# Prompt attention of a hybrid decoder layer: probabilities transposed in 32 by 32 blocks on VectorE and placed by DMAs through DRAM, in place of TensorE transposes

## The chip, the core and the metric

The kernel runs on one core of one Trainium2 chip. TensorE (PE) multiplies; VectorE (DVE), ScalarE (ACT) and GpSimd (POOL) do the rest; SyncE (SP) issues the weight loads. Each engine works through its own list of instructions in order, and semaphores hold an instruction until what it needs is there. The metric is the device time of one launch in microseconds; lower is better. The kernel before takes 1600.82 us (median of three runs, 1600.62 to 1601.08).

## The reference

One decoder layer for 256 prompt tokens and 64 sample tokens (8 sequences of 8). A combined projection gives the gates and inputs of a short convolution, and q, k, v of a sliding-window attention; two output projections, a merge, and a SwiGLU follow. What the change touches is the prompt's attention: 16 query heads, 4 key heads of width 64, in blocks of 128 queries, each of which sees its own block of keys and the one before.

```python
def window_attend(q, k, v, dist, valid, rel_bias, sinks):
    s = jnp.einsum('...qhgd,...shd->...hgqs', q, k).astype(jnp.float32) * (HEAD_DIM ** -0.5)
    bias = rel_bias.astype(jnp.float32)[t5_bucket(dist)]
    ...
    s = jnp.where(valid, s + bias, -jnp.inf)
    sink = sinks.astype(jnp.float32).reshape(N_KV_HEADS, GROUP, 1, 1)
    m = jnp.maximum(jnp.max(s, axis=-1, keepdims=True), sink)
    p = jnp.exp(s - m)
    p = p / (jnp.sum(p, axis=-1, keepdims=True) + jnp.exp(sink - m))
    return jnp.einsum('...hgqs,...shd->...qhgd', p.astype(v.dtype), v)
```

The scores `s` come out with queries on the partitions and keys along the row. The last product sums over keys, so the probabilities have to be turned: keys on the partitions.

## The kernel before

**Projections.** Every weight matrix is read once, in tiles of 4 x 128 rows by 256 columns. SP loads a tile as float32 (`wraw`, four buffers); ACT rounds it to the high part `whi` (L129) and VectorE subtracts to get the low part `wlo` (L130), three buffers of each. `product` (L172) then issues 24 matmuls on the tile: high part by the high and low parts of the activations, low part by the high part, 320 tokens wide. The projections run in the order q (four tiles per 256 columns), then four rounds of C, H, B (the convolution's inputs), then the gates and the output projections, then the feed-forward part.

**Side work.** After each tile `product` calls `tick`, which advances a generator by one step. While C, H and B run, that generator is the attention: its instructions are put between the tiles' matmuls on PE and between the `whi` and `wlo` on ACT and VectorE. The framework orders each engine's list by its own estimates, so that neighbours in the program may stand some places apart.

**The prompt's attention.** `prompt_attention` (L624) goes over eight units u0 to u7. A unit is one key head, two of its query heads and both query blocks: four 128 by 128 tiles of scores. A round of its loop takes two ticks. Per unit:

- `bias_load` (L530): GpSimd loads the relative biases (256 KB) one unit ahead.
- `prompt_scores` (L540): six matmuls into two PSUM banks, then four VectorE operations that add the biases. In the first query block each key row is used once; in the second, keys of the block before and of the own block are each masked out for half of the positions, and exactly one of the two is valid at each place, so the two are merged by a maximum into one 128 by 128 tile.
- `prompt_softmax` (L566): maximum on VectorE, four exponentials with their sums on ACT.
- `prompt_norm` (L585), one round later: division by the sums, four VectorE operations.
- `prompt_pt` (L591), one round after that: PE transposes the four tiles into the PSUM bank `pp`; ACT copies the first block's half into `pT`; VectorE multiplies the second block's half by the two masks `sides` (keys of the block before, keys of the own block), which undoes the merge and takes it to SBUF as well.
- `prompt_pv` (L605), for four units at a time: twelve matmuls by the values `vn` into two PSUM banks `po`, whose results ACT and VectorE split into the high and low rows of `at_t`.

```python
            if i >= 3 and (i - 3) % 4 == 3:
                for n in (i - 5, i - 3):
                    kv, gp = units[n]
                    prompt_pv(kv // 2, gp, (pts.pop(n - 1), pts.pop(n)))
```

The sample tokens' attention (L649) follows in the same generator and takes over the prompt's buffers. GpSimd also multiplies the convolution's rows by the norm (L829, L830), prepares the next rows (L811, L812) and keeps the state (L818, L819).

`vT` and `kT` (L277, L278) hold the transposed values and keys of all tokens. Their prompt part is read for the last time before the first unit (`kv_natural`, `keys_twice`); of `kT` the sample part is read later.

Of the kernel before, what the change touches and what calls it, by code (L numbers as in the profile page):

```python
# [8 lines left out]
F32 = mybir.dt.float32  # L9
F32R = mybir.dt.float32r  # L10
AF = mybir.ActivationFunctionType
# [5 lines left out]
TP, NB, TS = 256, 8, 8  # L17
T = TP + NB * TS
DC = 1024
NH, NKV, HD, GRP = 16, 4, 64, 4  # L20
DKV = NKV * HD
WIN = 128
# [4 lines left out]
P = 128  # L27
# [25 lines left out]
def hybrid_layer(ctx: ExitStack, tc: tile.TileContext, a: dict, o: list):  # L53
    nc = tc.nc
# [12 lines left out]
    dr = ctx.enter_context(tc.tile_pool(name="dr", bufs=1, space=bass.MemoryType.DRAM))  # L67
# [4 lines left out]
    def ps_aux(name):  # L72
        return aux[0].tile([P, 512], F32, tag="aux", name=name)
# [3 lines left out]
    def u(s):  # L77
        uid[0] += 1
        return f"{s}_{uid[0]}"
# [139 lines left out]
    ident = cst.tile([P, P], F32, name="ident")  # L219
# [57 lines left out]
    kT = zz.tile([P, 2, T], F32, name="kT")  # L277
    vT = zz.tile([P, 2, T], F32, name="vT")  # L278
    vn = [zz.tile([P, DKV], F32, name=f"vn{t}") for t in range(3)]
# [198 lines left out]
    pr = pr_p.enter_context(tc.tile_pool(name="pr", bufs=1, side="right"))  # L478
# [6 lines left out]
    sides = pr.tile([P, 2, WIN], F32, name="sides")  # L485
# [12 lines left out]
    def kv_natural(t):  # L498
        t0, tn = TOK[t]
        pk = ps_aux(u("pk"))  # L500
        for j in range(2):
            nc.tensor.transpose(pk[:tn, j * P:(j + 1) * P], vT[:, j, t0:t0 + tn], ident)
        if t > 0:
            for j in range(2):
                nc.tensor.transpose(pk[:tn, 256 + j * P:256 + (j + 1) * P], kT[:, j, t0:t0 + tn], ident)
        nc.vector.tensor_copy(vn[t][:tn, :], pk[:tn, 0:DKV])
        if t > 0:
            kn = pr.tile([P, 4, WIN], F32, tag="s", name=u("kn"), bufs=3).rearrange("p g k -> p (g k)")[:, :DKV]
            nc.vector.tensor_copy(kn[:tn, :], pk[:tn, 256:512])
            if t == 1:  # L510
                nc.gpsimd.dma_start(nk_p[0, 0].rearrange("t h d -> t (h d)"), kn)
                nc.gpsimd.dma_start(nv_p[0, 0].rearrange("t h d -> t (h d)"), vn[1])
            else:
                for dst, s in ((nk_s, kn), (nv_s, vn[2])):
                    nc.gpsimd.dma_start(
                        dst[0, :, WIN - TS:WIN].rearrange("b t h d -> b t (h d)"), s[:tn, :]
                    )
# [22 lines left out]
    def prompt_scores(kv, gp, bias):  # L540

        j, par = kv // 2, kv % 2
        s = pr.tile([P, 4, WIN], F32, tag="s", name=u("s"), bufs=3)
        ps1, ps0 = ps_aux(u("ps1")), ps_aux(u("ps0"))
        for gi in range(2):
            q = q2(j * 4 + gp * 2 + gi, par)
            for i in range(2):  # L550
                nc.tensor.matmul(
                    ps1[:, gi * 256:(gi + 1) * 256], q[:, WIN:2 * WIN], k2[:, kv, i], start=i == 0, stop=i == 1
                )
            nc.tensor.matmul(
                ps0[:, gi * 256:(gi + 1) * 256].rearrange("p (two k) -> p two k", two=2), q[:, 0:WIN],
                k2[:, kv, :, 0:WIN], start=True, stop=True,
            )
        w = pr.tile([P, 2, 2 * WIN], F32, tag="w", name=u("w"), bufs=1)
        nc.vector.tensor_add(w, ps1.rearrange("p (g k) -> p g k", g=2), flip(bias))
        nc.vector.tensor_max(s[:, 2:4], w[:, :, 0:WIN], w[:, :, WIN:2 * WIN])  # L560
        p0 = ps0.rearrange("p (g two k) -> p g two k", g=2, two=2)
        nc.vector.tensor_add(s[:, 0:2], p0[:, :, 0], flip(bias[:, :, 0:WIN]))
        nc.vector.tensor_add(s[:, 0:2], p0[:, :, 1], s[:, 0:2])
        return s

    def prompt_softmax(kv, gp, s):  # L566
# [15 lines left out]
        nc.scalar.activation(es, es, AF.Exp)  # L582
        return den, es

    def prompt_norm(s, den, es):  # L585
        nc.vector.tensor_add(den, den, es)
        nc.vector.reciprocal(den, den)
        for n in range(4):
            nc.vector.tensor_scalar(s[:, n], s[:, n], den[:, n // 2, n % 2:n % 2 + 1], None, op0=ALU.mult)

    def prompt_pt(s):  # L591
        pt = pr.tile([P, 3, 2 * WIN], F32, tag="pT", name=u("pT"), bufs=4)
        pp = ps_aux(u("pp"))
        for n in range(4):
            nc.tensor.transpose(pp[:, n * WIN:(n + 1) * WIN], s[:, n], ident)
        nc.scalar.activation(pt[:, 0, :], pp[:, 0:256], AF.Copy)
        for b in range(2):
            nc.vector.tensor_mul(
                pt[:, 1 + b, :].rearrange("p (g q) -> p g q", g=2),
                pp[:, 256:512].rearrange("p (g q) -> p g q", g=2),  # L600
                sides[:, b:b + 1].to_broadcast([P, 2, WIN]),
            )
        return pt

    def prompt_pv(j, gp, pts):  # L605
        po = ps_aux(u("po"))
        steps = ((0, 0, 0, True, True), (1, 0, 1, True, False), (1, 1, 2, False, True))
        for b, t, kb, st_, sp_ in steps:
            for par in range(2):
                kv = j * 2 + par  # L610
                nc.tensor.matmul(
                    po[par * 64:(par + 1) * 64, b * 256:(b + 1) * 256],
                    vn[t][:, kv * HD:(kv + 1) * HD], pts[par][:, kb, :], start=st_, stop=sp_,
                )
        for g in range(2):
            src = po.rearrange("p (b g s j) -> p g b s j", b=2, g=2, j=JS)[:, g]
            ch = j * 4 + gp * 2 + g
            two_to(*(x(ch)[:, 0:TP // JS, :].rearrange("p (b s) j -> p b s j", b=2) for x in (at_h, at_l)), src)
# [4 lines left out]

    def prompt_attention():  # L624
        units = [(j * 2 + par, gp) for j in range(2) for gp in range(2) for par in range(2)]
        bias, sc, sm, pts = {}, {}, {}, {}
        bias[0] = bias_load(*units[0])
        for i in range(len(units) + 3):
            if i < len(units):
                if i + 1 < len(units):  # L630
                    bias[i + 1] = bias_load(*units[i + 1])
                sc[i] = prompt_scores(*units[i], bias.pop(i))
                yield
                sm[i] = prompt_softmax(*units[i], sc[i])
            if i >= 3 and (i - 3) % 4 == 3:
                for n in (i - 5, i - 3):
                    kv, gp = units[n]
                    prompt_pv(kv // 2, gp, (pts.pop(n - 1), pts.pop(n)))
            if 0 <= i - 2 < len(units):
                pts[i - 2] = prompt_pt(sc.pop(i - 2))  # L640
            yield
            if 0 <= i - 1 < len(units):
                prompt_norm(sc[i - 1], *sm.pop(i - 1))
            if i >= len(units):
                yield

# [151 lines left out]
    for cp in range(4):  # L798
        c_sb = []
        ps = in_pair(O_C + cp * CW, "C")  # L800
        for c in range(2):
            t = tmp("ta", "csb")
# [472 lines left out]
```

## Time and profile before

| what | value |
|---|---|
| median of three runs | 1600.82 us |
| span of the profiled execution, first to last instruction | 1598.6 us |
| instructions | 26406 |
| granted TensorE clock, mean over the span | 0.998 |
| bytes moved by DMAs | 258.13 MB |
| share of the 16 DMA engines' span taken by GpSimd's queue | 1.3% |
| landing time of a 512 KB weight tile, median | 3.8 us |

The profile is one execution; of it the page gives the span, from the first instruction to the last, which lies 2.2 us under the median of the timed runs. Five columns of engines appear in it: PE for the matmuls, PEld for the loading of the stationary operand, DVE, ACT and POOL. "L186" is line 186 of the kernel. An engine's row shows the instruction's operands as out<-in by the program's names, its shapes, and in square brackets how long the engine had been idle and what ended that. PSUM and SBUF operands aren't told apart in the rows. Matmuls overlap, so what one of them costs is read from the distance between the starts of neighbours, not from its duration.

### The profile page before, as it was taken

The page shows a single profiled execution, that of the slowest core. Times are in us where ns is not written, and L with a number is a line of the kernel's source. Part 1 is how long each engine was busy: PE and PEld are TensorE (multiplying, and loading weights), DVE is VectorE, ACT ScalarE, POOL GpSimd, SP SyncE. Part 2 cuts the span into 40 slices and gives each one's busy share as a digit, 9 for nine tenths or more (in the row PEclk, how much of TensorE's full clock was granted, in tenths as well). Part 3 has the DMA queues.
Part 4 walks back from the last instruction along what each step waited for, and adds up shares of the span by engine and source line. Part 5 has one row for each costly group of instructions (what it writes and reads, how often), then busy time and mean ns, then how long its engine had stood idle before and what let it go on. Part 6 is the DMA issues. An engine that isn't in the chain of part 4 may idle for free.

```text
span 1598.6 us, 26406 instructions
## 1 busy us (share of the span) xinstructions
PE 1590.2 (99%) x10957; PEld 1554.8 (97%) x10957; DVE 884.0 (55%) x1315; ACT 650.6 (41%) x928; POOL 78.3 (5%) x123
## 2 busy tenths in 40 slices
PE   9999999999999999999999999999999999999998
PEld 9999999999999999999999999998888999999887
DVE  7879565445555545556555555553444455555556
ACT  7555433433333334444333333333333334444443
POOL 1101311000000003320000000000000000000000
PEclk9999999999999999999999999999999999999999
DMA  7554546545444444444445454455555445545552
GB/s 271 178 169 138 185 145 195 169 156 156 157 157 158 158 158 158 156 154 155 157 159 159 158 158 156 154 155 162 156 157 158 157 158 158 158 156 154 184 180 93
DMA packets 74399, 258.13 MB, mean 161 GB/s; under 512 B 8552, under 2 KB 11928, under 8 KB 74152
## 3 DMA queue, kind: packets, MB, share of 16 engines
q1 hardware_dynamic: 71880, 249.86, 49.4%
q0 software_dynamic: 1968, 5.90, 1.3%
q8 instruction: 86, 1.41, 0.4%
q10 hardware_dynamic: 432, 0.69, 0.1%
q14 instruction: 33, 0.27, 0.0%
HBM read 253.30 MB, written 5.08 MB: 162 GB/s over the span
## 4 chain that ended last, share of the span: by engine, by line
PE 99%; DVE 0%; ACT 0%; DVEq 0%; issue 0%
PE fu L186 18%; PE fg L186 18%; PE dn L970 9%; PE ga L186 7%; PE wo L186 7%; PE gc L186 7%; PE dn L978 6%; PE B L186 3%; PE C L186 3%; PE H L186 3%; PE q L186 3%; PE ya L186 3%; PE yc L186 3%; PE dl L974 2%; PE kv L376 2%; PE dn L1125 1%
## 5 line engine op out<-in xcount | busy, mean ns | idle before, releaser
L130 DVE TENSOR_TENSOR wlo<-wraw,whi 128x1024 fp32r<-128x1024 f32 (+1 forms) x460 | 561.7, 1222 | 585.4 <-ACT whi L129 470.0
L129 ACT ACTIVATE whi<-wraw 128x1024 fp32r<-128x1024 f32 (+1 forms) x460 | 485.5, 1056 | 720.4 <-PE fu L186 129.4
L186 PE MATMUL fu<-hh_t,whi 128*128 128x320 f32 x704 | 205.1, 301 | 0.0
L186 PE MATMUL fu<-hl_t,whi 128*128 128x320 f32 x704 | 205.1, 301 | 0.0
L186 PE MATMUL fg<-hl_t,whi 128*128 128x320 f32 x704 | 205.1, 301 | 0.0
L186 PE MATMUL fg<-hh_t,whi 128*128 128x320 f32 x704 | 205.1, 301 | 0.0
L186 PE MATMUL fu<-hh_t,wlo 128*128 128x320 f32 x704 | 158.9, 301 | 0.0
L186 PE MATMUL fg<-hh_t,wlo 128*128 128x320 f32 x704 | 158.9, 301 | 0.0
L970 PE MATMUL dn<-a_t,whi 128*128 128x512 f32 x640 | 155.4, 382 | 0.0
L186 PEld LDWEIGHTS fu<-hh_t,whi 128*128 128x128 f32 x704 | 131.8, 187 | 0.0
L186 PEld LDWEIGHTS fg<-hh_t,whi 128*128 128x128 f32 x704 | 131.8, 187 | 0.0
L186 PEld LDWEIGHTS fu<-hl_t,whi 128*128 128x128 f32 x704 | 131.8, 187 | 0.0
L186 PEld LDWEIGHTS fg<-hl_t,whi 128*128 128x128 f32 x704 | 131.8, 187 | 0.0
L970 PEld LDWEIGHTS dn<-a_t,whi 128*128 128x128 f32 x640 | 115.5, 187 | 16.3 <-issue 0.9
L186 PEld LDWEIGHTS fu<-hh_t,wlo 128*128 128x128 f32 x704 | 116.2, 187 | 0.0
L186 PEld LDWEIGHTS fg<-hh_t,wlo 128*128 128x128 f32 x704 | 116.2, 187 | 0.0
L978 PEld LDWEIGHTS dn<-a_t,wlo 128*128 128x128 f32 x640 | 97.7, 188 | 6.9
L978 PE MATMUL dn<-a_t,wlo 128*128 128x320 f32 x640 | 103.4, 301 | 0.0
L186 PE MATMUL wo<-m_l,whi 128*128 128x320 f32 x256 | 74.6, 301 | 0.0
L186 PE MATMUL ga<-xl_t,whi 128*128 128x320 f32 x256 | 74.6, 301 | 0.0
L186 PE MATMUL gc<-xl_t,whi 128*128 128x320 f32 x256 | 74.6, 301 | 0.0
L186 PE MATMUL wo<-m_h,whi 128*128 128x320 f32 x256 | 74.6, 301 | 0.0
(312 smaller groups left out, 2659.0 us busy)
## 6 DMA issues: line engine op xcount, KB each, us to landing
wraw<-in_w_in_dram SPq DMA_DIRECT2D x128, 512.0 KB, 3.8
wraw<-in_w_gate_dram SPq DMA_DIRECT2D x88, 512.0 KB, 3.7
wraw<-in_w_up_dram SPq DMA_DIRECT2D x88, 512.0 KB, 3.7
wraw<-in_w_down_dram SPq DMA_DIRECT2D x88, 512.0 KB, 3.7
wraw<-in_w_o_dram SPq DMA_DIRECT2D x32, 512.0 KB, 3.8
wraw<-in_w_conv_out_dram SPq DMA_DIRECT2D x16, 512.0 KB, 3.7
wraw<-in_w_attn_out_dram SPq DMA_DIRECT2D x16, 512.0 KB, 3.6
wraw<-in_w_kv_dram SPq DMA_DIRECT2D x6, 512.0 KB, 7.5
```

Of the source, the lines that this page charges most:

```text
L129: last["hi"] = nc.scalar.activation(hi, src, AF.Copy)
L130: last["lo"] = nc.vector.tensor_sub(lo, src, hi.bitcast(F32))
L186: last["mm"] = nc.tensor.matmul(turns(fives(ps[c][:, :T])), w[:, k, c * P:(c + 1) * P], turns(x(kc)), start=(kc == 0 and i == 0), stop=(kc ...
L376: last["mm"] = nc.tensor.matmul(turns(fives(ps[c][:, :T])), w[:, k, c * P:(c + 1) * P], turns(x(kc)), start=(kc == 0 and m == 0), stop=(kc ...
L970: nc.tensor.matmul(turns(placed(ps[c])), parts[k][0][:, cs], turns(a_move(k)), start=k == 0, stop=False)
L974: nc.tensor.matmul(low, a_low(k), parts[k][0], start=k == 0, stop=k == nf - 1 and c0 < E0)
L978: last["mm"] = nc.tensor.matmul(turns(placed(ps[c])[:, :, 0:JT]), parts[k][1][:, cs], turns(a_move(k)[:, :, 0:JT]), start=False, stop=k == ...
L1125: nc.tensor.matmul(turns(placed(ps[c])[:, :, JR:]), held[k][0][:, cs], turns(a_move(k)[:, :, JR:]), start=k == 0, stop=k == nf - 1,)
```

## The change

The transposes leave PE. `prompt_norm` now ends with one VectorE block transpose of the unit's four tiles: each 32 by 32 block is turned in place, into the first part of `vT`, which is free by then and serves as the one scratch of all units. A block that belongs to keys 32b to 32b+31 and queries 32a to 32a+31 then stands on the partitions of the queries' group a; it has to move to the partitions of group b. `blocks_out` does this by GpSimd's DMAs: the scratch goes to a DRAM buffer `scr` (256 KB, two buffers), and four loads, one for each group b of 32 partitions, bring it back into `pT` as 128 keys by 4 groups of 32 queries for each of the four tiles (runs of 512 bytes).

`prompt_sides` replaces the PSUM-to-SBUF step: the first block's half is used where it landed, and the second half is multiplied by the two masks in SBUF, once into `pm` (for every second pair of units into the free prompt part of `kT`) and once in place. `prompt_pv` reads the operand as groups of 32 queries.

The loop has one round more (`+ 4` for `+ 3`): the masks come two rounds after the normalization, and a group of value matmuls one round later than before. The scores' buffers `s` go from three to two, the `pT` buffers from four to six. Line numbers from L582 on are shifted: the normalization's division is L596, the block transpose L598, the store to DRAM L588, the loads L590, the masks L614 and L615, the value matmuls L624.

```diff
-            kn = pr.tile([P, 4, WIN], F32, tag="s", name=u("kn"), bufs=3).rearrange("p g k -> p (g k)")[:, :DKV]
+            kn = pr.tile([P, 4, WIN], F32, tag="s", name=u("kn"), bufs=2).rearrange("p g k -> p (g k)")[:, :DKV]
...
-        s = pr.tile([P, 4, WIN], F32, tag="s", name=u("s"), bufs=3)
+        s = pr.tile([P, 4, WIN], F32, tag="s", name=u("s"), bufs=2)
...
+    def blocks_out(dst, src):
+
+        scr = dr.tile([P, 4, dst.shape[2]], F32, tag=f"scr{dst.shape[2]}", name=u("scr"), bufs=2)
+        nc.gpsimd.dma_start(scr, src)
+        for b in range(4):
+            nc.gpsimd.dma_start(dst[32 * b:32 * b + 32], scr[:, b].rearrange("(a i) m -> i a m", a=4))
+
     def prompt_norm(s, den, es):
         nc.vector.tensor_add(den, den, es)
         nc.vector.reciprocal(den, den)
         for n in range(4):
             nc.vector.tensor_scalar(s[:, n], s[:, n], den[:, n // 2, n % 2:n % 2 + 1], None, op0=ALU.mult)
-
-    def prompt_pt(s):
-        pt = pr.tile([P, 3, 2 * WIN], F32, tag="pT", name=u("pT"), bufs=4)
-        pp = ps_aux(u("pp"))
-        for n in range(4):
-            nc.tensor.transpose(pp[:, n * WIN:(n + 1) * WIN], s[:, n], ident)
-        nc.scalar.activation(pt[:, 0, :], pp[:, 0:256], AF.Copy)
-        for b in range(2):
-            nc.vector.tensor_mul(
-                pt[:, 1 + b, :].rearrange("p (g q) -> p g q", g=2),
-                pp[:, 256:512].rearrange("p (g q) -> p g q", g=2),
-                sides[:, b:b + 1].to_broadcast([P, 2, WIN]),
-            )
+        x = vT.rearrange("p c t -> p (c t)")[:, :4 * WIN].rearrange("p (b m) -> p b m", b=4)
+        nc.vector.transpose(
+            x.rearrange("p b (n j) -> p n b j", n=4), s.rearrange("p n (b k) -> p n b k", b=4)
+        )
+        pt = pr.tile([P, 4, 4 * 32], F32, tag="pT", name=u("pT"), bufs=6)
+        blocks_out(pt, x)
         return pt
+
+    def prompt_sides(n, pt):
+        last2 = pt[:, :, 64:].rearrange("p a (g j) -> p a g j", g=2)
+        if n % 4 < 2:
+            pm = pr.tile([P, 4, 64], F32, tag="pm", name=u("pm"), bufs=2)
+        else:
+            pm = kT[:, n % 2, 0:TP].rearrange("p (a m) -> p a m", a=4)
+        parts = [
+            sides[:, b].rearrange("p (a j) -> p a j", a=4).unsqueeze(2).to_broadcast([P, 4, 2, 32]) for b in range(2)
+        ]
+        nc.vector.tensor_mul(pm.rearrange("p a (g j) -> p a g j", g=2), last2, parts[1])
+        nc.vector.tensor_mul(last2, last2, parts[0])
+        return pt[:, :, 0:64], pt[:, :, 64:], pm
...
                 nc.tensor.matmul(
-                    po[par * 64:(par + 1) * 64, b * 256:(b + 1) * 256],
-                    vn[t][:, kv * HD:(kv + 1) * HD], pts[par][:, kb, :], start=st_, stop=sp_,
+                    po[par * 64:(par + 1) * 64, b * 256:(b + 1) * 256].rearrange("p (g a j) -> p a g j", g=2, a=4),
+                    vn[t][:, kv * HD:(kv + 1) * HD], pts[par][kb].rearrange("p a (g j) -> p a g j", g=2),
+                    start=st_, stop=sp_,
                 )
...
-        bias, sc, sm, pts = {}, {}, {}, {}
+        bias, sc, sm, turned, pts = {}, {}, {}, {}, {}
         bias[0] = bias_load(*units[0])
-        for i in range(len(units) + 3):
+        for i in range(len(units) + 4):
...
-            if i >= 3 and (i - 3) % 4 == 3:
-                for n in (i - 5, i - 3):
+            if i >= 4 and i % 4 == 3:
+                for n in (i - 6, i - 4):
                     kv, gp = units[n]
                     prompt_pv(kv // 2, gp, (pts.pop(n - 1), pts.pop(n)))
-            if 0 <= i - 2 < len(units):
-                pts[i - 2] = prompt_pt(sc.pop(i - 2))
             yield
+            if 0 <= i - 3 < len(units):
+                pts[i - 3] = prompt_sides(i - 3, turned.pop(i - 3))
             if 0 <= i - 1 < len(units):
-                prompt_norm(sc[i - 1], *sm.pop(i - 1))
+                turned[i - 1] = prompt_norm(sc.pop(i - 1), *sm.pop(i - 1))
```

## The prediction

> **What bounds the kernel now.** I read the chain of waits and the engines' shares first, since they say whether any edit off the matrix engine can count.
>
> ```profile
> PE 1590.2 (99%) x10957; PEld 1554.8 (97%) x10957; DVE 884.0 (55%) x1315; ACT 650.6 (41%) x928; POOL 78.3 (5%) x123
> PE 99%; DVE 0%; ACT 0%; DVEq 0%; issue 0%
> ```
>
> The chain that ended last is matmul after matmul. Time leaves the kernel only where PE is given less work, and enters only where PE is made to wait. The next view splits the stretch in which the prompt's attention is woven into the projections (columns: PE, PEld, DVE, ACT, POOL busy).
>
> ```profile
> 100.00:140.00 40.00, 40.00 (x295) 39.99 (x294) 38.62 (x104) 22.23 (x64) 7.18 (x17) 1.00 0.55 170
> 140.00:160.00 20.00, 20.00 (x151) 18.70 (x150) 16.76 (x44) 9.94 (x29) 0.00 (x0) 1.00 0.35 114
> ```
>
> PE is full, and between 100 and 140 us VectorE is full too (38.62 of 40). Its 55% over the whole program hides that. VectorE also makes the low part of every weight tile (`wlo`, L130), without which PE cannot go on. The cover between the two is read from one tile, in the timeline (start, duration, engine, line):
>
> ```profile
> 110.32 1.06 ACT L129 ACTIVATE whi<-wraw 128x1024 fp32r<-128x1024 f32 x1 [2.98 <-PE H L186]
> 111.42 1.23 DVE L130 TENSOR_TENSOR wlo<-wraw,whi 128x1024 fp32r<-128x1024 f32 x1
> 118.93 0.39 PE L186 MATMUL B<-xh_t,whi 128*128 128x320 f32 x1
> ```
>
> Three buffers are turned over, so this tile is B's first, used from 118.93 on. Its low part was ready at 112.65, and its eight leading matmuls use only the high part (8 x 0.14 = 1.1 us): 7.4 us of cover. VectorE may be that late before PE notices.
>
> **The change part by part.** *PE, removed.* Each of the 8 units (4 heads-by-query-block tiles each; u0 to u7) gave PE four transposes:
>
> ```profile
> 163.73 0.58 PE L186 MATMUL H<-xh_t,wlo 128*128 128x320 f32 x3
> 164.15 0.60 PE L595 MATMUL pp<-ident,s 128*128 128x128 f32 x4
> 164.50 0.39 PE L186 MATMUL H<-xh_t,whi 128*128 128x320 f32 x1
> 164.73 0.31 PE L186 MATMUL H<-xl_t,whi 128*128 128x320 f32 x1
> 164.87 0.30 PE L186 MATMUL H<-xh_t,whi 128*128 128x320 f32 x1
> L595 PE MATMUL pp<-ident,s x32: 270/272/331, 110.7 to 164.5; 128*128 128x128 f32 x32
> ```
>
> Without the group, H's first matmul would start at 164.15 and its second 0.14 us later, at 164.29; it started at 164.73. A group costs 0.44 us, and 32/4 = 8 groups cost 3.5 us. All of it is on the path, so 3.5 us is also the most that can be won.
>
> *PE, altered.* The value matmuls (L611) now read their moving operand in runs of 32 numbers. The projections in the rows above read in runs of 4 and go at 0.14 us per 320 columns, so I take nothing; the bound above is a doubling of
>
> ```profile
> 142.43 2.81 PE L611 MATMUL po<-pT,vn 128*64 128x256 f32 x24
> ```
>
> twice, 5.5 us. *ACT* loses eight copies from PSUM; ACT was half idle, so nothing.
>
> *VectorE, added.* A block transpose of 128x512 per unit, which no row shows. The nearest are operations that read as many numbers:
>
> ```profile
> L571 DVE TENSOR_REDUCE mx<-s 128x4 f32<-128x512 f32 x8 | 5.5, 682 | 0.1
> L560 DVE TENSOR_TENSOR s<-w 128x256 f32<-128x256 f32 x8 | 3.5, 434 | 0.0
> L598 DVE TENSOR_TENSOR pT<-pp,sides 128x256 f32<-128x256 f32 x14 | 5.3, 415 | 0.0
> L130 DVE TENSOR_TENSOR wlo<-wraw,whi 128x1024 fp32r<-128x1024 f32 x18 | 22.0, 1223 | 4.1 <-ACT whi L129 3.8
> ```
>
> I take 0.7 us; below, 0.42 (as for half the numbers), above, 1.22 (as for twice). The two mask products cost as much from SBUF (434 ns) as from PSUM (415). So VectorE gets 8 x 0.7 = 5.6 us more in a stretch where it has 4.6 us free (60 minus 38.62 and 16.76).
>
> The Trainium skill, VectorE: DVE Perf Modes, section "The three transpose paths", speaks against the change: it lists 390 ns on TensorE and 311 on VectorE for 128x128 in bf16 and advises TensorE for a full 128x128 transpose. An estimate from that page is 4 x 311 = 1.24 us a unit, which would put the sum at the third case below; the trace's four TensorE transposes in 0.44 us disagree with the page's 4 x 390 ns, and no row shows the VectorE one.
>
> *GpSimd, added.* Per unit a 256 KB store to DRAM and, after it has landed, four 64 KB loads, on the queue that also carries the bias loads. Columns: KB each, us from issue to landing; then the issue's own ns.
>
> ```profile
> bias<-e_scr POOLq DMA_DIRECT2D x8, 256.0 KB, 4.1
> kf<-in_cache_kt_dram POOLq DMA_DIRECT2D x4, 256.0 KB, 5.0
> bias_s<-e_scr POOLq DMA_DIRECT2D x1, 68.0 KB, 2.9
> out_dram<-kn POOLq DMA_DIRECT2D x1, 64.0 KB, 3.6
> L511 POOL DMA_DIRECT2D out_dram<-kn x1 | 0.6, 553 | 0.0
> ```
>
> I take 4.1 for the store, 0.57 per issue and 3.6 for a load: from the end of the transpose to the last block in place 4.1 + 3 x 0.57 + 3.6 = 9.4 us, and 4.1 + 4 x 0.57 = 6.4 us of the queue. Bounds: 2.9 for loads that meet no queue, 5.0 for every landing as for the four `kf` loads in a row. A round of the loop takes PE two tiles and one set of scores, 2 x 3.36 + 0.71 = 7.4 us, and the masks come two rounds after the transpose, so in the middle the 9.4 us are mostly covered. They are not at the end, where nothing but the queue separates the last units. VectorE's instructions from unit 7's normalization on stood before as
>
> ```order
> L586 TENSOR_TENSOR den_1971<-den_1971,es_1972 128x4
> L587 RECIPROCAL den_1971<-den_1971 128x4
> L589 TENSOR_SCALAR s_1926<-s_1926,den_1971 128x128 x4
> L130 TENSOR_TENSOR wlo_2119<-wraw_2116,whi_2118 128x1024
> L598 TENSOR_TENSOR pT_2032<-pp_2033,sides 128x256 x2
> L130 TENSOR_TENSOR wlo_2177<-wraw_2174,whi_2176 128x1024
> ```
>
> and stand now (s_1816 is u6, s_1917 u7; vT the scratch; pT_2040 and pT_2087 their placed blocks)
>
> ```order
> L598 STREAM_TRANSPOSE vT<-s_1816 128x4x4x32
> L615 TENSOR_TENSOR pT_1910<-pT_1910,sides 128x4x64
> L593 TENSOR_TENSOR den_1962<-den_1962,es_1963 128x4
> L130 TENSOR_TENSOR wlo_2127<-wraw_2124,whi_2126 128x1024
> L594 RECIPROCAL den_1962<-den_1962 128x4
> L596 TENSOR_SCALAR s_1917<-s_1917,den_1962 128x128 x4
> L598 STREAM_TRANSPOSE vT<-s_1917 128x4x4x32
> L130 TENSOR_TENSOR wlo_2187<-wraw_2184,whi_2186 128x1024
> L130 TENSOR_TENSOR wlo_2217<-wraw_2214,whi_2216 128x1024
> L614 TENSOR_TENSOR kT<-pT_2040,sides 128x256
> ```
>
> Behind the second transpose, which must wait until u6's store has left the one scratch, stand the `wlo` of B's second round; behind u6's mask, which must wait for u6's loads, stand the next. On GpSimd's queue the order is now
>
> ```order
> L588 DMA scr_2041<-vT 128x512
> L590 DMA pT_2040<-scr_2041 32x4x128 x4
> L588 DMA scr_2088<-vT 128x512
> L590 DMA pT_2087<-scr_2088 32x4x128 x4
> L832 COPY g_494<-ue_2156 128x2
> ```
>
> so u7's store goes out only when u6's four loads are issued.
>
> *The walk to the end of it.* In VectorE's timeline before, the stretch from H's third `wlo` to unit 7's scores, and the idle in it:
>
> ```profile
> 105.10 1.22 DVE L130 TENSOR_TENSOR wlo<-wraw,whi 128x1024 fp32r<-128x1024 f32 x1
> 113.06 0.17 DVE L586 TENSOR_TENSOR den<-den,es 128x4 f32<-128x4 f32 x1 [0.42 <-ACT es L582]
> 115.27 1.22 DVE L130 TENSOR_TENSOR wlo<-wraw,whi 128x1024 fp32r<-128x1024 f32 x1 [0.40 <-ACT whi L129]
> 144.94 0.16 DVE L586 TENSOR_TENSOR den<-den,es 128x4 f32<-128x4 f32 x1 [0.44 <-ACT es L582]
> 149.86 1.22 DVE L130 TENSOR_TENSOR wlo<-wraw,whi 128x1024 fp32r<-128x1024 f32 x1 [1.79 <-ACT whi L129]
> 151.00 0.68 DVE L559 TENSOR_TENSOR w<-ps,bias 128x512 f32<-128x512 f32 x1
> ```
>
> It is 45.9 us with 3.05 idle, 42.85 of work. Now six transposes come in (4.2), and four copies of value results (1.3), one pair of masks (0.65) and one `wlo` (1.13) move behind it: 44.0, plus waits for u0's loads of about 1.6 us (its masks stand two `wlo` behind u1's transpose). Unit 7's scores are then added at 105.1 + 45.6 = 150.7, as late as before although PE has saved time. The 8.9 us of work that follow in the order bring u6's transpose to about 160, ending 160.7. Then: store landed 164.9; u7's transpose ends 165.6; u6's loads issued by 167.2, u7's store landed 171.3, its last load 171.3 + 1.7 + 3.6 = 176.6; a mask, a `wlo` and a mask more, 178.6.
>
> PE without any wait: B's second round began at 168.00 and its value matmuls at
>
> ```profile
> 168.00 0.30 PE L186 MATMUL B<-xh_t,whi 128*128 128x320 f32 x1
> 171.51 2.81 PE L611 MATMUL po<-pT,vn 128*64 128x256 f32 x24
> ```
>
> which now stand two tiles later: 171.5 + 6.7 - 3.5 = 174.7, and the part that reads u7's masks comes 16 of the 24 matmuls (1.8 us) later, 176.5. PE waits 178.6 - 176.5 = 2.1 us. On the way, B's first `wlo` ends at 166.8 where PE wants it at 168.0 - 3.5 + 1.1 = 165.6, 1.2 us late; that wait is part of the 2.1, since it moves PE by as much. The sum: 1598.6 - 3.5 + 2.1 = 1597.2 against the profile's own span, and with the 2.2 us that the median of 1600.82 lies above the span, 1599.4 us. At both ends of the unknown prices: landings of 5.0 lengthen the tail by 0.9 + 0.9 + 1.4 and u5's loads ahead of it by 2.3, so 7.6 us of wait and 1604.9; the slow transpose adds 7 x 0.54, so 1603.2; the short prices leave no wait, 1597.3.
>
> **The rivals.** *All hidden.* Loads of 2.9, stores of 3.6 and a transpose of 0.42 shorten the tail by 0.5 + 0.5 + 0.7 + 0.6, more than 2.1: 1597.3. For it: `bias_s`; against: `kf`, and VectorE's fullness. The Trainium skill, DMA: Bandwidth & Descriptors, section "Anatomy of one DMA", fits 2.0 us plus bytes/436e3, an estimate of 2.6 us for 256 KB; by that rule this case holds. The trace's 4.1 disagrees.
>
> *VectorE and the queue become the bound.* With a transpose of 1.0 us or more, or landings near 5.0 (four loads in a row look like `kf`), the low parts come late from C's second round on, and PE loses 6 to 9 us: about 1605, slower. It decides from a loss of 3.5 + 3.2 on.
>
> *The strided value matmuls run at half rate*: 1599.4 + 5.5 = 1604.9. Against it stand the projections' runs of 4.
>
> **How the numbers follow.** Forecast 0.45, all hidden 0.24, VectorE and queue bound 0.27, strided 0.04. A change of 0.2% is 3.2 us, about what a measurement of this kernel can tell. The forecast's own range, 1597.8 to 1603.5, lies within that; all hidden is just beyond it in 0.20 of its 0.24; the last two are slower. Faster 0.20, same 0.49, slower 0.31. The range 1597.2 to 1605 takes in the gain's limit and one slow price, not both.
>
> **What would show it.** No L595 on PE, and tiles that follow each other without the 0.44 us. A STREAM_TRANSPOSE near 0.7 us. VectorE waiting for the loads before u0's, u6's and u7's masks; PE waiting near 165 and before the last value matmuls, 2 us in all. VectorE fuller than 38.62 of 40 from 100 to 140. I am wrong if PE waits for `wlo` already before 150 us, if its waits exceed 6 us, or if a store and its loads take less than 8 us.

## The result, and the profile after

The change makes the kernel slower by some 5 us, about 0.4%; the forecast was 1599.4 us.

| kernel | timed runs, us | span of the profiled run |
|---|---|---|
| before | 1600.87 median (1600.09 to 1601.08) | 1598.6 |
| changed | 1604.42, 1604.99, 1605.63, 1607.44, 1611.77 | 1605.7 |
| ratio | 1.0038, 95% interval 1.0027 to 1.0049 | |

A sixth timing of the changed kernel, 4216.09 us, is a disturbed run and is left out of what follows; with it the median is 1606.54, without it 1605.63. The profiled run is the one of 1607.44.

First the page's shares, then its chain of waits.

```profile
PE 1591.2 (99%) x10925; PEld 1553.2 (97%) x10925; DVE 887.1 (55%) x1323; ACT 647.4 (40%) x920; POOL 100.9 (6%) x163
PE 95%; DMA 2%; POOL 1%; issue 1%; DVE 1%; ACT 0%; DVEq 0%; POOLq 0%
```

PE has lost its 32 transposes (10957 to 10925), VectorE has eight instructions more. The chain, which before was PE to 99%, now runs 5% of the span over DMAs, VectorE and GpSimd: for 1300 of its 1600 us the program is as it was, and in the attention it hangs on the new way through DRAM. The view of PE's waits (total, times, longest; the one at the start of the program is left out) says how often:

```profile
PE C L186 <- DVE wlo L130: 2.1, 1, 2.1
PE B L186 <- DVE wlo L130: 2.0, 2, 1.4
PE po L624 <- DVE pT L615: 1.3, 1, 1.3
PE po L624 <- DMA pT<-scr: 0.8, 1, 0.8
```

That is 6.2 us in all, counted from the end of the matmul before. Before there was no such wait. The longest, followed back in VectorE's timeline and PE's (start, duration, in brackets the idle before):

```profile
143.87 0.70 DVE L598 STREAM_TRANSPOSE vT<-s 128x512 f32<-128x512 f32 x1
147.13 0.42 DVE L614 TENSOR_TENSOR kT<-pT,sides 128x256 f32<-128x256 f32 x1 [2.56 <-DMA pT<-scr]
148.88 1.22 DVE L130 TENSOR_TENSOR wlo<-wraw,whi 128x1024 fp32r<-128x1024 f32 x1
```

```profile
147.78 0.30 PE L186 MATMUL C<-xl_t,whi 128*128 128x320 f32 x1
150.15 0.83 PE L186 MATMUL C<-xh_t,wlo 128*128 128x320 f32 x4 [2.07 <-DVE wlo L130]
```

VectorE stands 2.56 us before u3's masks, since the loads are not there. Five vector operations and then the low part that PE wants from 147.9 on stand behind the first of those masks. PE is still for 2.07 us.

A second loss follows, which no list of waits shows. Windows of 2 us (columns: PE busy, PEld, DVE, ACT, POOL, then the granted clock):

```profile
148.00:150.00 2.00, 0.08 (x1) 0.00 (x0) 2.00 (x5) 0.00 (x0) 1.04 (x2) 1.00 0.01 2
150.00:152.00 2.00, 1.85 (x11) 1.85 (x12) 2.00 (x6) 0.01 (x1) 1.14 (x3) 0.84 0.63 182
152.00:154.00 2.00, 2.00 (x9) 1.63 (x9) 1.97 (x7) 2.00 (x10) 0.14 (x1) 0.50 0.93 270
154.00:156.00 2.00, 2.00 (x18) 1.20 (x16) 2.00 (x6) 1.63 (x2) 0.43 (x1) 0.81 0.83 303
...
184.00:186.00 2.00, 0.71 (x6) 0.29 (x4) 2.00 (x4) 0.00 (x0) 0.00 (x0) 0.87 0.00 0
186.00:188.00 2.00, 2.00 (x7) 0.86 (x5) 2.00 (x3) 0.00 (x0) 0.88 (x2) 0.50 0.73 236
188.00:190.00 2.00, 2.00 (x12) 2.00 (x12) 1.11 (x3) 1.22 (x5) 2.00 (x3) 0.77 0.83 229
```

Between 152 and 154 us PE runs at half clock: the projections' matmuls start 0.27 us apart (151.67, 151.93, 152.20) and not 0.14. In each of the two places the clock lost is (0.16 + 0.50 + 0.19) x 2 and (0.13 + 0.50 + 0.23) x 2, 1.7 us both times. It happens after the wait of 2.07 us and after the pair of 0.79 and 1.29 us that lie within 2 us of each other. The waits of 1.38 and 0.65 us near 124 and 133 left the clock at 1.00. The Trainium skill, TensorE: Matmul & The Clock Gate, section "HAM oscillation — how this bites in real kernels", warns of idle gaps over some 3.4 us; here 2.07 us were enough, so the measurement decides for a shorter gap. The window of 3413 ns that the Trainium skill gives in Part 1 of the same page does agree with the length of the dip: 1.7 us lost at half clock is 3.4 us.

The ledger of the profiled run: 3.5 saved, 6.2 waited, 2 x 1.7 lost to the clock, +6.1 together; the span grew by 7.1. The missing 1 us is in the way of counting the waits. A matmul lasts 0.3 us and its neighbour starts 0.14 us after it, so a wait counted from a matmul's end is too short by the overlap. From start to start the five waits are 1.69, 0.95, 2.37, 1.17 and 1.67 us (at 122.68, 131.87, 147.78, 182.60 and 184.04); less the usual distances of 0.14 and, for the value matmuls, 0.11 us, that is 7.2 us, and the ledger comes to +7.1.

This run is the slowest of the changed kernel but for the one at 1611.77. Its mean granted clock is 0.997; that of the four others is 0.998 or 0.999, so they probably lost less to the clock. No trace of them was kept.

Why the loads are late, in GpSimd's timeline and VectorE's for u0, whose block transpose ended at 105.2:

```profile
105.53 0.59 POOL L588 DMA_DIRECT2D scr<-vT  x1 [3.60 <-DVE vT L598]
111.15 2.18 POOL L590 DMA_DIRECT2D pT<-scr  x4 [5.03 <-DMA scr<-vT]
```

```profile
118.06 0.43 DVE L614 TENSOR_TENSOR pm<-pT,sides 128x256 f32<-128x256 f32 x1 [3.93 <-DMA pT<-scr]
L598 DVE STREAM_TRANSPOSE vT<-s 128x512 f32<-128x512 f32 x8 | 5.7, 707 | 1.5 <-DMA scr<-vT 1.4
```

From the store's issue to the first load's 5.6 us, three more issues of 0.55 behind it, and 5.3 us from the last one's start to the masks: 12.5 us for what was put at 9.4. (u0 and u7 have the longest ways of the eight; the average stands in the account of the prediction, below.) The block transposes themselves (the last row, from the groups of VectorE) take 707 ns, as forecast.

### The profile page after: what moved, and what is told of

Read it like the earlier page. It is cut to its first block, busy times and chain, and to the rows that moved or that the text cites. A ratio compares the mean times of both kernels' runs of the same rounds, so it can differ in the third digit from the quotient of the medians.

```text
span 1605.7 us, 26425 instructions
## 1 busy us (share of the span) xinstructions
PE 1591.2 (99%) x10925; PEld 1553.2 (97%) x10925; DVE 887.1 (55%) x1323; ACT 647.4 (40%) x920; POOL 100.9 (6%) x163
## 4 chain that ended last, share of the span: by engine, by line
PE 95%; DMA 2%; POOL 1%; issue 1%; DVE 1%; ACT 0%; DVEq 0%; POOLq 0%
PE fu L186 18%; PE fg L186 18%; PE dn L984 9%; PE wo L186 7%; PE ga L186 7%; PE gc L186 7%; PE dn L992 6%; PE q L186 3%; PE ya L186 3%; PE yc L186 3%; PE C L186 3%; PE H L186 2%; PE B L186 2%; PE dl L988 2%; PE kv L376 2%; DMA pT<-scr 1%
## 5 line engine op out<-in xcount | busy, mean ns | idle before, releaser
L186 PE MATMUL gc<-xh_t,whi 128*128 128x320 f32 x256 | 74.5, 301 | 0.0
L186 PE MATMUL ga<-xh_t,whi 128*128 128x320 f32 x256 | 74.5, 301 | 0.0
```

The lines of the kernel that those rows point to most:

```text
L186: last["mm"] = nc.tensor.matmul(turns(fives(ps[c][:, :T])), w[:, k, c * P:(c + 1) * P], turns(x(kc)), start=(kc == 0 and i == 0), stop=(kc ...
```

## Experiments

All were timed in five rounds beside the kernel before; the table gives all of them, the sections what they say. A row stands for ten to twelve timings, e9's for five. The nudge in some of the names is one lone matmul, explained in the third group.

| kernel | median, us (range) | ratio to before, 95% |
|---|---|---|
| e1_no_dma | 1604.30 (1603.95 to 1604.71) | 1.0023 (1.0014 to 1.0032) |
| e2_transposes_too | 1600.47 (1599.94 to 1601.17) | 1.0000 (0.9991 to 1.0008) |
| e3_dmas_too | 1600.30 (1600.11 to 1601.01) | 0.9998 (0.9989 to 1.0007) |
| e4_one_round_later | two groups: 1598.43 to 1600.11, 1606.50 to 1607.86 | 1.0017 (1.0003 to 1.0031) |
| e5_sp_queue | 1604.16 (1603.72 to 1604.55) | 1.0023 (1.0013 to 1.0032) |
| e7_no_dma_nudge | 1597.61 (1597.01 to 1597.90) | 0.9981 (0.9972 to 0.9990) |
| e8_later_nudge | 1600.42 (1599.87 to 1601.72) | 0.9999 (0.9990 to 1.0008) |
| e9_change_nudge | 1605.87 (1604.85 to 1606.88) | 1.0032 (1.0019 to 1.0045) |
| e10_sp_later_nudge | 1597.46 (1596.75 to 1597.90) | 0.9978 (0.9969 to 0.9987) |
| e11_sp_nudge | 1597.58 (1597.04 to 1598.35) | 0.9980 (0.9972 to 0.9989) |
| e12_before_nudge | 1600.86 (1600.26 to 1601.81) | 1.0001 (0.9992 to 1.0010) |
| e13_store_sp_nudge | 1601.19 (1600.31 to 1601.94) | 1.0005 (0.9996 to 1.0014) |

### Is it VectorE's work, or the traffic?

**e2_transposes_too**: the kernel before, with the eight block transposes added, unread.

```diff
+        x = vT.rearrange("p c t -> p (c t)")[:, :4 * WIN].rearrange("p (b m) -> p b m", b=4)
+        nc.vector.transpose(
+            x.rearrange("p b (n j) -> p n b j", n=4), s.rearrange("p n (b k) -> p n b k", b=4)
+        )
```

> The kernel before with the eight block transposes added on VectorE, their result read by nobody; PE's transposes stay. Late blocks: 1601 to 1602 us, the 7 us of cover take 5.7 us of work. VectorE full: 1605 or more, PE waits for wlo between 110 and 150 us. DMA traffic: 1601.

**e3_dmas_too**: the kernel before, with the store and the four loads of each unit on GpSimd's queue, into dead space.

```diff
+        x = s.rearrange("p n k -> p (n k)").rearrange("p (b m) -> p b m", b=4)
+        scr = dr.tile([P, 4, 128], F32, tag="scr128", name=u("scr"), bufs=2)
+        nc.gpsimd.dma_start(scr, x)
+        dead = vT.rearrange("p c t -> p (c t)")[:, :4 * WIN].rearrange("p (b m) -> p b m", b=4)
+        for b in range(4):
+            nc.gpsimd.dma_start(dead[32 * b:32 * b + 32], scr[:, b].rearrange("(a i) m -> i a m", a=4))
```

> The kernel before with the store and the four loads per unit added on GpSimd's queue, into a place that nobody reads. Late blocks and VectorE full: 1600.9 within 0.6 us, since no engine but GpSimd waits for them. DMA traffic: 1604 or more, weight tiles landing later than 3.8 us, or waits for biases.

Both run as fast as before, 1600.47 and 1600.30; e2 is even under the 1601 to 1602 that late blocks alone were expected to make of it. VectorE's 5.7 us in its fullest stretch cost nothing, and 40 more transfers cost nothing, as long as nobody waits for either. So what costs is the wait that ties them to VectorE's list.

### Without the placing, and with more time for it

**e1_no_dma**: block transposes straight into `pT`; the placing by DMAs is left out.

```diff
-        x = vT.rearrange("p c t -> p (c t)")[:, :4 * WIN].rearrange("p (b m) -> p b m", b=4)
+        pt = pr.tile([P, 4, 4 * 32], F32, tag="pT", name=u("pT"), bufs=6)
         nc.vector.transpose(
-            x.rearrange("p b (n j) -> p n b j", n=4), s.rearrange("p n (b k) -> p n b k", b=4)
+            pt.rearrange("p b (n j) -> p n b j", n=4), s.rearrange("p n (b k) -> p n b k", b=4)
         )
-        pt = pr.tile([P, 4, 4 * 32], F32, tag="pT", name=u("pT"), bufs=6)
-        blocks_out(pt, x)
```

> The change without its DMAs: VectorE transposes straight into pT, nothing moves the blocks to their partitions, so the placing is left out of what is computed. Late blocks (VectorE waits for the loads, and the low parts of the weights queue behind the masks): 1597 to 1599 us, no PE wait for wlo. VectorE full (the eight transposes, 5.7 us on an engine with 4.6 us free, are the price): 1603 or more, with the waits for wlo still there. DMA traffic (the added transfers slow the weight tiles): 1597 to 1599.

**e4_one_round_later**: masks three rounds after the transpose instead of two, the value matmuls a round later.

```diff
-        for i in range(len(units) + 4):
+        for i in range(len(units) + 5):
...
-            if i >= 4 and i % 4 == 3:
-                for n in (i - 6, i - 4):
+            if i >= 8 and i % 4 == 0:
+                for n in (i - 7, i - 5):
...
-            if 0 <= i - 3 < len(units):
-                pts[i - 3] = prompt_sides(i - 3, turned.pop(i - 3))
+            if 0 <= i - 4 < len(units):
+                pts[i - 4] = prompt_sides(i - 4, turned.pop(i - 4))
```

> The change with the masks three rounds after the normalization instead of two, and the value matmuls one round later. Late blocks: about 11 us of transfers fit into 22 us, the waits before the masks go, 1597.3 to 1599.5 us. VectorE full or DMA traffic: no better than the change, 1605 to 1607.

Neither went as the wait alone would have it. e1's PE has no wait at all in the attention and 32 transposes less, and yet e1 takes 1604.3 us. e4 falls into two groups 8 us apart. The chain of waits of e1 (start, duration, line, count), and under it one piece of the chain before:

```profile
596.59 109.23 PE wo L186 x768
705.81 13.65 PE fg L186 x96
719.47 0.32 PE pss L211 x2
719.78 0.15 PE nudge L207
719.93 13.44 PE fu L186 x96
733.37 13.44 PE fg L186 x96
```

```profile
594.48 107.52 PE wo L186 x768
```

The same 768 matmuls, in code the change doesn't touch and without a wait, take 109.23 us in e1 and 107.52 before: 142.2 ns each against 140.0. At 719.78 stands `nudge`, a lone matmul that the program has there, and from it on e1 too goes at 13.44 us for 96. In e4's profiled run, one of the upper group, the same piece also takes 109.23 us. PE has two paces for the same stream of matmuls. Which of them it is left with when the attention's side work ends differs from kernel to kernel, in e4 from run to run, and in these profiles it holds until the next nudge.

### The pace, tried by moving a nudge forward

The same edit in four kernels: one nudge before the first gate product, at about 268 us instead of 720.

```diff
         for nm, off, tag in (("gc", O_GC, "ta"), ("ga", O_GA, "tb")):
+            if (mp, nm) == (0, "gc"):
+                nudge(xh, xl)
             ps = in_pair(off + c0, nm)
```

> As e1_no_dma (block transposes straight into pT, the placing by DMAs left out), with one lone matmul (`nudge`) before the first gate product of the first half. Pace theory: after the side matmuls of attention the stream of products goes on at 142.2 ns per matmul instead of 140.0 until the next lone matmul, and that is all that e1 lost; with a lone matmul some 480 us earlier it gets most of its 7 us back: 1596.5 to 1598.0 us, with 140.0 ns behind the new nudge. Rival, that what e1 left out changes the work after it in some other way: 1603.5 to 1605 as e1 was, with 142.2 ns behind the nudge too.

> As e4_one_round_later, with a nudge before the first gate product. Pace theory: the two groups of e4 (six runs at 1598.4 to 1600.1, six at 1606.5 to 1607.9) become one at 1598.4 to 1600.5, since the slow pace now ends at the new nudge. Rival, that the upper group is made of waits in attention: both groups stay, half of the runs above 1606.

> The changed kernel with a nudge before the first gate product, nothing else. Pace theory: the profiled run of the change was at 140.0 ns behind attention, its loss comes of the waits for wlo and pT and of the lower clock behind them, so the median stays at 1604 to 1606 and only values like 1611.8 vanish. Rival, that most of the loss in the timed runs is pace as in e1: 1598 to 1601.

> The kernel before with the same nudge added. Pace theory: it already runs at 140.0 ns behind attention, so 1600.8 plus at most 0.3 us, 1600.5 to 1601.3. Rival, that a nudge at this place is worth something by itself whatever the attention does: under 1599.

The medians of all four came out as the pace theory has it, though five of e8's eleven timings lie above its 1600.5, by up to 1.2 us. e7 falls by 6.7 us against e1, to 1597.61. From 268.5 to 719.8 us, at 142.2 ns apart, about 3170 matmuls lie, and 3170 x 2.2 ns is 7.0. The turn itself, in e7's chain:

```profile
241.15 13.65 PE H L186 x96
254.80 13.66 PE B L186 x96
268.46 0.14 PE nudge L207
268.60 13.45 PE gc L186 x96
282.05 13.44 PE ga L186 x96
```

e12, the control, is unchanged: the kernel before was already at 140.0. e8 loses e4's upper group. e9 takes as long as the change itself. The change's profiled run was at 140.0 behind the attention (the 768 `wo` matmuls took 107.52 us there too), so the pace is not what made that run slow. e9's profiled run was at 142.2 there, up to the nudge:

```profile
264.42 13.65 PE B L186 x96
278.22 13.44 PE gc L186 x96
```

So the change can leave the attention at either pace, and without the nudge this run would have lost some 7 us more. The value of 1611.77 among the change's timings fits one run at the slower pace (1604.4 + 7), but no profile of such a run was taken, and with five timings of each kernel its absence from e9 says little.

e9 against e7 is now the price of the way through DRAM, 1605.87 - 1597.61 = 8.3 us. Between the two profiled runs it is 9.5 us, and no dip of the clock is in it: e9's waits are 7.4 us from start to start, and up to the first gate product its projections' matmuls lie 142.3 ns apart on average where e7's lie 141.4, another 1.3 us. And e8 is still at 1600.42. Its profiled run, the slowest of the eleven (1601.72), has one wait, PE's 2.0 us for a low part of B at 133 us, with the clock behind it:

```profile
PE B L186 <- DVE wlo L130: 2.0, 1, 2.0
...
134.00:136.00 2.00, 2.00 (x11) 2.00 (x10) 2.00 (x8) 2.00 (x9) 0.00 (x0) 0.64 0.95 195
136.00:138.00 2.00, 2.00 (x9) 2.00 (x9) 2.00 (x5) 0.96 (x2) 0.58 (x1) 0.51 1.02 418
```

In this run 2.0 of wait and (0.36 + 0.49) x 2 = 1.7 of clock eat the 3.5 that the transposes gave.

### The same transfers on another queue

**e11_sp_nudge** is e9 with store and loads issued by SP, **e10_sp_later_nudge** is e8 with the same edit, **e13_store_sp_nudge** is e9 with the first of the two lines alone, and **e5_sp_queue** is e11 without the nudge.

```diff
-        nc.gpsimd.dma_start(scr, src)
+        nc.sync.dma_start(scr, src)
...
-            nc.gpsimd.dma_start(dst[32 * b:32 * b + 32], scr[:, b].rearrange("(a i) m -> i a m", a=4))
+            nc.sync.dma_start(dst[32 * b:32 * b + 32], scr[:, b].rearrange("(a i) m -> i a m", a=4))
```

> e9_change_nudge (the change and a nudge) with the store and the four loads of each unit issued on SP's queue instead of GpSimd's. Wait theory: the loss of e9 against e7 (8.3 us) is the time from block transpose to masks, in which VectorE stands still and holds back the low parts; GpSimd waits 22.6 us in all for the stores of the change and takes up to 5.6 us for a store and 5.3 us for a load. If SP's landings take 2.5 to 3.5 us as its weight loads do in the profile before, VectorE's waits fall to under 1.5 us each, PE waits under 2 us in all: 1597.5 to 1600.5. Rival, that the landing is the same on every queue (it is the way through DRAM that takes 4 to 5 us): 1604 to 1607 as e9. Second rival, that SP's waits hold back the weight loads behind them: PE waits for xh or weights, over 1607.

> e8_later_nudge (masks three rounds after the transpose, value matmuls a round later, nudge) with store and loads on SP's queue. Wait theory: e8's one wait of PE for a low part (2.05 us at 133 us, with the halved clock after it about 4 us) comes of VectorE standing behind the first masks; with shorter landings it is gone and the time is near e7's 1597.6: 1597.3 to 1599.0. Rival, landing the same on every queue: 1600 to 1601.5 as e8. Second rival, weight loads held back: over 1602.

e11 takes 1597.58, e10 1597.46: both 0.2% faster than the kernel before, and as fast as e7 without any placing. PE has no wait left in the attention. u0's way in e11, SP's timeline and VectorE's:

```profile
105.88 0.33 SPq L588 DMA_DIRECT2D scr<-vT  x1
109.69 1.75 SPq L590 DMA_DIRECT2D pT<-scr  x4
```

```profile
114.74 0.43 DVE L614 TENSOR_TENSOR pm<-pT,sides 128x256 f32<-128x256 f32 x1 [1.10 <-DMA pT<-scr]
```

Store to load 3.8 us instead of 5.6, four issues in 1.75 instead of 2.18 us, the masks 3.3 us after these instead of 4.7: 8.9 us from store to masks where the change takes 12.5. But u0 shows more than the other units. Over all eight, from the end of the block transpose to the landing of the last block, the way takes 8.8 us on average in e11 and 11.3 in e9. The landings (KB each, median us from issue to landing), e9's first:

```profile
scr<-vT POOLq DMA_DIRECT2D x8, 256.0 KB, 3.5
pT<-scr POOLq DMA_DIRECT2D x32, 64.0 KB, 4.1
```

```profile
scr<-vT SPq DMA_DIRECT2D x8, 256.0 KB, 3.7
pT<-scr SPq DMA_DIRECT2D x32, 64.0 KB, 3.6
```

A store lands no sooner on SP's queue. Of the 2.5 us, the landing of the fourth load has 1.3 (4.6 to 3.3 on average). The steps between have most of the rest: 0.4 from the transpose's end to the store's issue, 0.3 from the store's landing to the first load, 0.4 in the loads' issues. On GpSimd's queue u1's and u7's stores stood behind the loads of the unit before and went out 1.7 and 1.9 us after their transposes. The weight loads on SP's queue do not suffer visibly (no wait of PE follows from them), though eight stores and 32 loads now stand among them; the 2.5 to 3.5 us that the expectation names as their landing before is too short, the profile before has medians of 3.6 to 3.8 us for all but six of them.

The Trainium skill, DMA: Bandwidth & Descriptors, section "Issuing engine by pattern", names Sync for a plain load or store and calls that way generally faster than GpSimd's. The medians above agree for the loads and not for the stores. The 0.4 us between the first-byte figures that the Trainium skill gives on the same page under "Specifications" (about 1 and 0.6 us) is near the 0.5 us of the loads; but in e13, below, loads on GpSimd's queue land in 3.4 us in the median, so the queue alone does not set it.

> e9_change_nudge with the store alone on SP's queue, the loads on GpSimd's. Wait theory: from the first unit's block transpose to its masks e9 takes some 13 us and e11 some 9.5; the store has about half of the difference, so VectorE's waits for pT and PE's for wlo shrink by about half against e9: 1599.5 to 1602.5. Rival, that SP's queue helps by another way than the shorter chain (GpSimd freed of its wait for the store): the loads' part is kept as in e9 and the time is above 1603.5, or all is gained with the store alone, under 1598.5.

> The changed kernel with store and loads on SP's queue, no nudge: e11_sp_nudge without its nudge. Pace theory: PE does not wait in attention, as in e1 and e11, so the stream is left at 142.2 ns as in e1 and loses about 7 us until the old nudge at 719 us: 1603.8 to 1605.0 although no wait is left. Rival, that the pace in e1 came of the left-out placing alone: 1597 to 1598 as e11.

e13 lies between, at 1601.19; the masks of u0 run at 115.75, and PE's waits shrink to two:

```profile
PE B L186 <- DVE wlo L130: 1.1, 1, 1.1
PE C L186 <- DVE wlo L130: 1.1, 1, 1.1
```

So the time goes with the length of the chain, step by step: 12.2 us from u0's store to its masks in e9, 9.9 in e13, 8.9 in e11 (from transpose to last landing, on average over the units, 11.3, 9.9 and 8.8), for 1605.87, 1601.19 and 1597.58. How much of e13's gain is shorter landings and how much is that its stores no longer stand behind loads on GpSimd's queue, these runs do not separate. e5 has no wait of PE either and still takes 1604.16, as the pace theory said. At 300 to 310 us its clock stands at 1.00, so the pace is not the granted clock:

```profile
300.00:310.00 10.00, 10.00 (x73) 10.00 (x72) 5.94 (x9) 3.07 (x5) 0.00 (x0) 1.00 0.48 154
```

A faster queue alone would thus not have made the change faster than before; it takes the nudge as well.

## Why the prediction was wrong

**Right.** *What PE gains*: e11's span is 2.7 us under before's (1595.9 to 1598.6). The 3.5 us are in it to 0.2 us, less one nudge (0.15) and about 0.5 for the other pace, at which more of e11's matmuls go: from 95 to 290 us the undisturbed stretches of the stream cost 1.1 us over 140.0 ns per matmul in e11 and 0.65 before. *The value matmuls* cost nothing more: a group of 24 takes 2.74 us from its start to the next matmul's, before (142.43 to 145.17) and in e11 (148.12 to 150.86); the fourth case falls. *The block transpose*: 707 ns forecast as 0.7. VectorE's added work and the transfers as such cost nothing (e2, e3). *The waits* before u0's, u6's and u7's masks are where they were put (3.93, 4.21 and 3.33 us). And the way of thinking held: with the blocks in place after 8.8 us PE does not wait (e11), after 9.9 it waits twice (e13), after 11.3 and 11.6 five times and more (e9 and the change).

**The step that failed** is the price of the way through DRAM: from the end of a block transpose to the last block in place 4.1 + 3 x 0.57 + 3.6 = 9.4 us. In the change it took 11.6 us on average over the eight units, from 9.8 for u6 to 14.4 for u7. The store was priced well (3.85 us on average, though 5.2 to 5.3 for u0, u1 and u7), and so were the issues (1.8). The last load landed after 4.8 us on average and not after 3.6. The row that was nearest in kind, four loads in a row at 5.0, was kept as the bound and not taken. And two hand-overs had been put at nothing: 0.7 us from the transpose's end to the store's issue, 0.4 from the store's landing to the first load. With 11.6 us the sentence "in the middle the 9.4 us are mostly covered" falls too: the wait before u0's masks was 3.93 instead of 1.6, u3's and u5's masks had waits of 2.56 and 2.91 us that the walk did not have at all, and PE waited at 124, 133, and 150 us, not at the tail alone. u7's masks ran from 183.75 to 185.65, not to 178.6.

The 7.4 us of cover for a low part were real, and they were used up at B's second tile. VectorE's timeline in the change, then PE's:

```profile
110.96 0.71 DVE L598 STREAM_TRANSPOSE vT<-s 128x512 f32<-128x512 f32 x1 [1.24 <-DMA scr<-vT]
123.09 1.23 DVE L130 TENSOR_TENSOR wlo<-wraw,whi 128x1024 fp32r<-128x1024 f32 x1
```

```profile
124.37 0.41 PE L186 MATMUL B<-xh_t,wlo 128*128 128x320 f32 x1 [1.38 <-DVE wlo L130]
```

The low part of this tile ran at 115.27 us before and runs at 123.09 now, 7.8 us later. The wait before u0's masks has 3.93 of that, the wait of u1's transpose until u0's store had left the one scratch 1.24, and the transposes and masks in front of it the rest.

Two of the signs of being wrong that the prediction named came: a wait of PE for `wlo` before 150 us, and more than 6 us of them. One of the signs of being right did not: VectorE was not fuller from 100 to 140 us but emptier, 34.73 of 40, because it stood waiting.

The third case, "VectorE and the queue become the bound", had the right trigger (landings near 5.0), nearly the right time (1605) and 0.27. Its 6 to 9 us of loss hold for the waits (7.2 us from start to start); that the clock's part is not in them makes the time partly luck. It was wrong on where it starts, with B in the first round and not with C in the second, and on "VectorE full": it is VectorE's waiting, not its work, as e2 shows.

**Not thought of.** The prediction's first step, that time enters only where PE is made to wait, put two terms at nothing. PE can pay for a wait twice: 1.7 us of clock in each of two places, 3.4 of the profiled run's loss. And the stream behind the attention may go on at another pace: every sum took the 140.0 ns of before for granted. "All hidden, 1597.3" was the right figure for a change whose transfers are hidden (1597.6 in e7 and e11), but only with a nudge behind it; without one, such a kernel takes 1604.2 (e5). The forecast's own 1599.4 would have been missed at either pace. Two small slips changed little. The 2.2 us from span to time pairs a span with a median of other runs; a run of the kernel before at 1600.46 us has a span of 1598.6, 1.9 us less, and the changed kernel's profiled run lies 1.7 us over its span. The slow transpose's 0.54 goes with 1.24 us and not with the stated bound of 1.22: 7 x 0.52 gives 1603.0, not 1603.2.

**Open.** What sets the pace that the attention leaves behind. Kernels without any wait (e1, e5) end at 142.2 in their profiles, and their timings, all within 0.9 us, leave no room for the other pace; e4, with one wait, does either. The four profiled kernels that keep the transposes on PE (before, e2, e3, e12) all leave the attention at 140.0, and of the ten without them nine leave it at 142.2, the change's profiled run alone at 140.0. So taking the transposes off PE may be what brings the slower pace, but no run tries that by itself. Nor is it one switch: the pace changes at several groups of side matmuls. At the last of these, the sample tokens' value matmuls, e11 goes from 140.1 to 142.2 ns (before and behind 221 to 224 us), while the kernel before stays at 140 there. That a nudge ends the slower pace is shown; why, and why the interruptions by attention matmuls sometimes do the same, is not.

## What to carry to other kernels

A transfer that an in-order engine waits for delays everything behind that wait: measure the chain from store to use on the queue that will carry it, hand-overs included and for every unit, and compare it with the cover of the next thing in that engine's list, not of the wait's own result. A gap of about 2 us in a stream of matmuls can cost nearly twice its length, through the clock, as it did in three places here. And when a long untouched stretch changes its time, compare the time of one group of equal matmuls in both profiles before explaining the difference by the edit.

## What the hardware showed unexpectedly

- The same plain transfers, a store and four loads behind it, are ready 2.5 us sooner on SP's queue than on GpSimd's (8.8 against 11.3 us on average from transpose to last block, e11 and e9), which is worth 8.3 us of the kernel. The store's landing has no part in it (medians of 3.7 and 3.5 us).
- Half the granted clock for 3.4 us after idle gaps of 2.07, 2.05 and 0.79 + 1.29 us; none after e4's 1.78 us (1.00 in each window of 2 us from 130 to 140) and none in e9, whose longest was 1.7. Whether the length of the gap alone decides, these few cases do not show.
- Two paces of the same matmul stream at a granted clock of 1.00, 140.0 and 142.2 ns per 320 columns, lasting for hundreds of microseconds and ended by one lone matmul.
